# One encoder layer in float32: the first of the seven block products of the middle FFN pairs written as 512-column matmuls

## The chip, the cores and the metric

The kernel runs on one core of a Trainium2 chip. The metric is the device time of one execution in microseconds (us), as the median of several runs. A difference of about 0.2% (2.1 us) is what a measurement of this kernel can tell from none.

## The reference

One layer of a bidirectional encoder on 512 tokens of width 1024, all in float32. The change lies in the two feed-forward networks (FFN), one before and one after the attention part:

```python
def _swiglu(x, w_gate, w_up, w_down):
    return (jax.nn.silu(x @ w_gate) * (x @ w_up)) @ w_down

f = _swiglu(_rmsnorm(x, ffn1_pre_g[l]), ffn1_w_gate[l], ffn1_w_up[l], ffn1_w_down[l])
x = x + 0.5 * _rmsnorm(f, ffn1_post_g[l])
...   # attention branches, gates, output projection
f = _swiglu(_rmsnorm(x, ffn2_pre_g[l]), ffn2_w_gate[l], ffn2_w_up[l], ffn2_w_down[l])
x = x + 0.5 * _rmsnorm(f, ffn2_post_g[l])
```

`D_FF` is 2816, so each FFN has 22 blocks of 128 hidden features, and each block needs a piece of the gate weights and a piece of the up weights (a "pair").

## The kernel before

**Precision by splitting.** A float32 value is split into a high part `hi` (a cast to fp32r, done by ScalarE in line 113) and a low part `lo = x - hi` (VectorE, line 114). A product is the sum of high times high, high times low, and low times high: the helper `mm3` (lines 204 to 206) issues these as three matmuls.

**Seven products instead of eight.** For 20 of the 22 pairs of each FFN, `seven` computes the 2x2 block product (gate and up rows against two halves of 256 tokens, over two halves of the contraction) with seven block products after Strassen and Winograd. Product `i` of pair `j` multiplies a sum of weight blocks by a sum of token blocks; 1, 2 and 4 use the plain tokens (`hn` in the names), the others use sums (`v`). The products add up in three PSUM banks per pair: `q` takes 1, 6, 7 and 4, `p` takes 5 and 3, and `r` takes 2. A pair's products 7 and 4 are issued in the next pair's pass, so one pass over `j` issues: product 1 of `j`; 7 of `j-1` with 5 of `j`; then 2 and 6 of `j`, 4 of `j-1`, 3 of `j`.

**Narrow and wide.** A product has four contraction steps of 128. Narrow, it is 4 times `mm3` with 256 columns: twelve matmuls. Wide, the high weights multiply `[hi|lo]` of the tokens in one 512-column matmul per step (line 461), and the low weights multiply `hi` in one 256-column matmul per step (line 464): eight matmuls. High times low then lies in columns 256 to 511 of the bank and must be added to the rest by VectorE. `run` issues the 512-column halves of the products of one call first, then their 256-column halves. In each FFN, product 2 is wide for `j` from 4 to 16, and products 3, 5, 6, 7 and 4 in most pairs; product 1 is narrow everywhere.

**What follows a product.** After product 1, ScalarE copies `q[:, :256]` to `g` (line 495), from which the gate value of one token half is made; the same bank then goes on adding up products 6, 7 and 4. Line 506 on VectorE subtracts `q` (after product 7) from the copy `p5` of product 5, for the pair before; line 507 adds that sum's two halves; line 521 adds the two halves of `r` to `g`; line 536 subtracts the copy of `q` from `p`; line 638 multiplies gate and up. Lines 410 and 415 (`sums_of`) form weight sums for the next pair; lines 113 and 114 split the weight blocks.

**What sets the order.** TensorE's order inside `seven` is the order of the code, kept by manual dependencies. The order of VectorE and ScalarE is decided at build time by a scheduler with a model of its own. Each engine executes its list strictly in that order, and an instruction at the head of a list that waits on a semaphore holds all behind it.

Of the kernel before, what the change touches and what calls it, by code (L numbers as in the profile page):

```python
# [16 lines left out]
ALU = mybir.AluOpType  # L17
# [7 lines left out]
NF = 2816 // P  # L25
# [1 line left out]
EPS = 1e-6  # L27
NEG = -1.0e30
NUNIT = 38
WIDE = (5, 2, 6, 3, 7, 4)  # L30
PIECE = 1024
NPIECE = 6
SPREAD = 4
# [2 lines left out]
STD = 2  # L36
EARLY = 4
# [9 lines left out]
def block_kernel(ctx, tc, x, gains, weights, rpb_near, rpb_all, alibi0, alibi12, out):  # L47
    nc = tc.nc
# [12 lines left out]
    def unit(dt=F32, name="u"):  # L61
        return up.tile([P, 512], dt, tag="u", name=name)

    def twin(name):
        return up.tile([P, PIECE], F32R, tag="twin", name=name, bufs=8)
# [54 lines left out]
    state = {"used": False, "next": 0, "take": 0, "stop": EARLY + 2 * STD, "ahead": lambda: None}  # L120
# [231 lines left out]
    def combined():  # L352
# [17 lines left out]
        for n, of in ((5, lambda i: (whole[0][i], whole[1][i], sub)), (6, lambda i: (v[5][i], a[0][i], sub)),  # L370
# [5 lines left out]
            for i in range(2):  # L376
                if n in WIDE:
                    t = twin("v").rearrange("p (k s t) -> p k s t", k=2, s=2)
# [10 lines left out]
    def load_blocks(n0, j):  # L389

        w11, t1, t3 = unit(name="w11"), unit(name="t1"), unit(name="t3")
        gate, up = (n0 + j, n0 + EARLY + 2 * STD + j) if j < EARLY else [n0 + 2 * STD + 2 * j + i for i in range(2)]
        nc.sync.dma_start(t1, weights[up][:, :512])
        nc.sync.dma_start(t3, weights[up][:, :512])
        raw = {3: w11, 5: t1, 7: t3}
        if j < EARLY:
            raw[4] = unit(name="t4")
            nc.sync.dma_start(raw[4], weights[gate][:, 512:])
        else:
            r = wp.tile([P, PIECE], F32, tag="raw", name="raw", bufs=2)  # L400
            nc.sync.dma_start(r, weights[gate])
            raw[1], raw[2] = r[:, :512], r[:, 512:]
        nc.sync.dma_start(w11, weights[up][:, 512:])
        nc.gpsimd.dma_start(t1, weights[gate][:, :512], accum_op=ALU.add)  # L404
        nc.gpsimd.dma_start(t3, weights[up][:, 512:], accum_op=ALU.add)
        return raw

    def sums_of(raw):
        raw[6] = unit(name="t2")
        nc.vector.tensor_tensor(raw[6], raw[5], raw[3], op=ALU.add)  # L410
        if 4 in raw:
            nc.vector.tensor_tensor(raw[4], raw[6], raw[4], op=ALU.add)
        else:
            raw[4] = unit(name="t4")
            nc.vector.tensor_tensor(raw[4], raw[6], raw[2], op=ALU.add)

    def split_block(raw):
        w = wp.tile([P, PIECE], F32R, tag="w", name="w")
        split(w[:, :512], w[:, 512:], raw)
        return w  # L420

    def seven(use, mv, n_pairs, n0, behind, far, lead, raws, early, put, pin):

        blocks = {}
        o = {}

        def get(j):
            if j < n_pairs and j > 2:
                raws[j] = load_blocks(n0, j)
            if j >= n_pairs - 1:
                behind(far)

        def ready(j, i):
            if j < n_pairs:
                if j and loads:
                    loads.popleft()()  # L440
                if i == 1:
                    sums_of(raws[j])
                if j >= EARLY or i not in (1, 2):
                    blocks[j, i] = split_block(raws[j].pop(i))
            else:
                behind(lead)

        def product(j, i, key, start):
            if start:
                o[key, j] = bank(key)  # L450
            w = blocks.pop((j, i))
            high = [w[:, k * P:(k + 1) * P] for k in range(4)]
            low = [w[:, 512 + k * P:512 + (k + 1) * P] for k in range(4)]
            acc = o[key, j][:, :256]
            if i not in WIDE or j not in state["wide"] or (key in "qr" and j < EARLY) or (i == 2 and j > NF - STD - 4):
                for k in range(4):
                    mm3(acc, high[k], low[k], *mv[i][k][:2], start and k == 0, k == 3, skip_group_check=True)
                return
            for k in range(4):
                to = shaped(o[key, j], mv[i][k][2])  # L460
                nc.tensor.matmul(to, high[k], mv[i][k][2], start=start and k == 0, stop=False, skip_group_check=True)  # L461
            yield
            for k in range(4):
                nc.tensor.matmul(acc, low[k], mv[i][k][0], start=False, stop=k == 3, skip_group_check=True)  # L464

        def run(*products):
            products = [product(*p) for p in products]
            for _ in range(2):
                for p in products:
                    next(p, None)  # L470

        def full(j):
            return j in state["wide"] and j >= EARLY

        res = {}
        get(0)
        get(1)
        blocks[0, 5] = split_block(raws[0][5])
        ready(0, 1)
        raws[0].pop(5)  # L480
        for i in (6, 3, 7, 4):
            ready(0, i)
            if i == 3:
                put()
        begin = mark()
        for j in range(n_pairs + 1):
            now, was = j < n_pairs, j > 0
            get(j + 2)
            if now:
                if j < EARLY:  # L490
                    o["q", j], g = early[j]
                else:
                    run((j, 1, "q", True))
                    g = unit(name="g")
                    nc.scalar.copy(g[:, :256], o["q", j][:, :256])
                u = unit(name="up")
                res[j] = g, u, unit(name="p5") if j in state["wide"] else u[:, 256:]
            ready(j + 1, 1)
            if pin and j == 0:
                pool.append((pin, mark(), (mybir.EngineType.DVE,)))  # L500
            run(*[(j - 1, 7, "q", False)] * was, *[(j, 5, "p", True)] * now)
            if was:
                g0, u0, s0 = res.pop(j - 1)
                q0 = o["q", j - 1]
                if full(j - 1):
                    nc.vector.tensor_tensor(s0, s0, q0, op=ALU.subtract)
                    nc.vector.tensor_tensor(u0[:, 256:], s0[:, :256], s0[:, 256:], op=ALU.add)
                else:
                    nc.vector.tensor_tensor(u0[:, 256:], s0[:, :256], q0[:, :256], op=ALU.subtract)
                if j - 1 in state["wide"] and not full(j - 1):  # L510
                    nc.vector.tensor_tensor(u0[:, 256:], u0[:, 256:], s0[:, 256:], op=ALU.add)
            ready(j + 1, 5)
            if now:
                p = o["p", j]
                nc.scalar.copy(res[j][2], p if j in state["wide"] else p[:, :256])
            ready(j + 1, 2)
            two = now and j >= EARLY
            run(*[(j, 2, "r", True)] * two, *[(j, 6, "q", False)] * now, *[(j - 1, 4, "q", False)] * was, *[(j, 3, "p", False)] * now)
            if two:
                for part in range(1 + (full(j) and j <= NF - STD - 4)):  # L520
                    nc.vector.tensor_tensor(g[:, :256], g[:, :256], o["r", j][:, part * 256:part * 256 + 256], op=ALU.add)
            ready(j + 1, 6)
            if now:
                nc.scalar.copy(u if full(j) else u[:, :256], o["q", j] if full(j) else o["q", j][:, :256])
            ready(j + 1, 3)
            if was:
                if full(j - 1):
                    nc.scalar.copy(g0[:, 256:], q0[:, 256:])
                    nc.vector.tensor_tensor(g0[:, 256:], q0[:, :256], g0[:, 256:], op=ALU.add)
                    use(j - 1, g0, u0, g0[:, 256:])  # L530
                else:
                    use(j - 1, g0, u0, q0[:, :256])
            ready(j + 1, 7)
            if now:
                if full(j):
                    nc.vector.tensor_tensor(u, p, u, op=ALU.subtract)
                    nc.vector.tensor_tensor(u[:, :256], u[:, :256], u[:, 256:], op=ALU.add)
                else:
                    nc.vector.tensor_tensor(u[:, :256], p[:, :256], u[:, :256], op=ALU.subtract)
                if j in state["wide"] and not full(j):  # L540
                    nc.vector.tensor_tensor(u[:, :256], p[:, 256:], u[:, :256], op=ALU.add)
            ready(j + 1, 4)
        pool.append((begin, mark(), (mybir.EngineType.PE,)))
# [1256 lines left out]
```

## Time and profile before

| | |
|---|---|
| median of 3 runs | 1069.86 us (1069.64 to 1069.97) |
| profiled execution, its own time | 1070.8 us |
| span of that execution in the trace | 1069.0 us |
| granted TensorE clock | 0.998 |
| TensorE matmul busy | 1061.0 us (99% of the span), 5955 matmuls |
| VectorE busy | 871.1 us (81%) |
| ScalarE busy | 653.0 us (61%) |
| pairs `j` = 4 to 16 of the first FFN | about 72 to 200 us of the span |
| pairs `j` = 4 to 16 of the second FFN | about 798 to 925 us of the span |

The span is what the trace covers; the execution's own time is 1.8 us longer. Matmul records overlap (a 256-column matmul is recorded with 0.28 us, while the next one starts 0.12 us after it), so the time that a matmul costs is read from start to start. The same holds for VectorE's records: a 128x256 addition is recorded with 0.42 us, and the next one may start 0.33 us after its start.

### The profile page before, as it was taken

How to read it: one execution, taken by the hardware profiler on the slowest of the kernel's cores; microseconds unless marked ns; L12 is line 12 of the kernel's file. 1: busy time of each engine (PE TensorE's matmuls, PEld its weight loads, DVE VectorE, ACT ScalarE, POOL GpSimd, SP SyncE). 2: the span in 40 equal slices, each digit the busy share in tenths (PEclk: the TensorE clock that was granted, in tenths of full speed). 3: DMA queues.
4: the chain of work that ended last, by engine and by line, in shares of the span. 5: the costliest groups of instructions: out<-in, count | busy, mean ns of one | idle time of the engine just before them, and what ended most of it. 6: DMA issues, size and time to landing. Idle time of an engine off the chain costs nothing.

```text
span 1069.0 us, 17160 instructions
## 1 busy us (share of the span) xinstructions
PE 1061.0 (99%) x5955; PEld 926.4 (87%) x5955; DVE 871.1 (81%) x1694; ACT 653.0 (61%) x1348; POOL 193.1 (18%) x253
## 2 busy tenths in 40 slices
PE   9999999999999999999999999999999999999997
PEld 7898988998888988888988888889899899988886
DVE  7998999989987666676777644777998999989985
ACT  7656656566674655577766641366655566667671
POOL 4111211024334000000000001043311111124331
PEclk9999999999999999999999999999999999999999
DMA  9899987779993444322233239595947678869952
GB/s 331 188 231 234 235 206 200 197 182 264 248 311 118 154 158 164 116 68 74 80 89 97 79 106 308 148 199 186 286 100 197 158 198 204 216 203 234 217 195 79
DMA packets 98027, 193.95 MB, mean 181 GB/s; under 512 B 24338, under 2 KB 26898, under 8 KB 97939
## 3 DMA queue, kind: packets, MB, share of 16 engines
q1 hardware_dynamic: 69760, 138.37, 38.8%
q0 software_dynamic: 25488, 54.01, 28.3%
q8 instruction: 47, 0.77, 0.3%
q10 hardware_dynamic: 2690, 0.46, 0.2%
q14 instruction: 42, 0.34, 0.1%
HBM read 185.68 MB, written 9.68 MB: 183 GB/s over the span
## 4 chain that ended last, share of the span: by engine, by line
PE 92%; DMA 4%; DVE 2%; ACT 0%; issue 0%; SPq 0%; DVEq 0%; ACTq 0%
PE ps L204 10%; PE ps L206 10%; PE ps L205 10%; PE q L461 7%; PE q L206 6%; PE q L204 6%; PE q L205 6%; PE p L461 6%; PE q L464 4%; PE p L464 3%; PE c L206 2%; PE c L204 2%; PE c L205 2%; PE r L461 2%; PE r L204 1%; PE r L206 1%
## 5 line engine op out<-in xcount | busy, mean ns | idle before, releaser
L114 DVE TENSOR_TENSOR w<-raw,w 128x512 fp32r<-128x512 f32 (+1 forms) x142 | 129.8, 919 | 70.9 <-ACT w L113 68.2
L113 ACT CAST w<-t 128x512 fp32r<-128x512 f32 x160 | 98.0, 622 | 115.1 <-DVE t L410 62.6
L113 ACT CAST w<-raw 128x512 fp32r<-128x512 f32 (+1 forms) x142 | 114.1, 809 | 78.9 <-PE ps L205 31.9
L204 PE MATMUL ps<-hn,w 128*128 128x512 f32 (+1 forms) x360 | 136.5, 379 | 0.0
L206 PE MATMUL ps<-hn,w 128*128 128x512 f32 (+1 forms) x360 | 134.6, 374 | 0.0
L205 PE MATMUL ps<-hn,w 128*128 128x512 f32 (+1 forms) x360 | 134.3, 373 | 0.0
L114 DVE TENSOR_TENSOR w<-t,w 128x512 fp32r<-128x512 f32 x160 | 108.3, 685 | 1.0 <-ACT w L113 0.8
L404 POOL DMA_DIRECT2D t<-in_weights_dram x40 | 35.0, 875 | 286.1 <-DVE w L114 58.5
L206 PEld LDWEIGHTS ps<-hn,w 128*128 128x128 f32 x360 | 67.8, 188 | 12.7 <-DVE w L114 0.7
L204 PEld LDWEIGHTS ps<-hn,w 128*128 128x128 f32 x360 | 67.9, 189 | 11.4
L205 PEld LDWEIGHTS ps<-hn,w 128*128 128x128 f32 x360 | 67.9, 189 | 10.9
L461 PE MATMUL p<-v,w 128*128 128x512 f32 x272 | 73.1, 390 | 0.0
L113 ACT CAST w<-room 128x1024 fp32r<-128x1024 f32 x49 | 51.5, 1052 | 31.7 <-PE q L206 7.8
L114 DVE TENSOR_TENSOR w<-room,w 128x1024 fp32r<-128x1024 f32 x49 | 59.6, 1220 | 7.3 <-ACT w L113 4.1
L461 PE MATMUL q<-v,w 128*128 128x512 f32 x240 | 65.1, 392 | 0.0
L750 POOL DMA_DIRECT2D room<-in_weights_dram x7 | 6.1, 873 | 320.5 <-DMA room<-in_weights_dram 313.9
L461 PEld LDWEIGHTS p<-v,w 128*128 128x128 f32 x272 | 50.4, 188 | 10.2
L731 POOL DMA_DIRECT2D rows<-in_weights_dram x36 | 37.0, 1251 | 95.0 <-DVE w L114 61.6
L461 PEld LDWEIGHTS q<-v,w 128*128 128x128 f32 x240 | 43.0, 189 | 7.5
L113 ACT CAST w<-rows 128x512 fp32r<-128x512 f32 x62 | 36.0, 618 | 20.7 <-PE q L206 9.5
L206 PE MATMUL q<-hn,w 128*128 128x256 f32 x168 | 47.5, 283 | 0.0
L205 PE MATMUL q<-hn,w 128*128 128x256 f32 x168 | 47.5, 283 | 0.0
(334 smaller groups left out, 3066.0 us busy)
## 6 DMA issues: line engine op xcount, KB each, us to landing
raw<-in_weights_dram SPq DMA_DIRECT2D x94, 512.0 KB
t<-in_weights_dram SPq DMA_DIRECT2D x88, 256.0 KB
t<-in_weights_dram POOLq DMA_DIRECT2D x80, 256.0 KB, 5.7
room<-in_weights_dram SPq DMA_DIRECT2D x37, 512.0 KB
room<-in_weights_dram POOLq DMA_DIRECT2D x29, 512.0 KB, 11.9
w<-in_weights_dram SPq DMA_DIRECT2D x40, 256.0 KB
rows<-in_weights_dram POOLq DMA_DIRECT2D x36, 256.0 KB, 8.7
w<-in_weights_dram POOLq DMA_DIRECT2D x32, 256.0 KB, 9.1
```

Source lines behind the costliest of these rows:

```text
L113: nc.scalar.copy(hi, src)
L114: nc.vector.tensor_tensor(lo, src, hi.bitcast(F32), op=ALU.subtract)
L204: nc.tensor.matmul(o, sh, mh, start=start, stop=False, **kw)
L205: nc.tensor.matmul(o, sh, ml, start=False, stop=False, **kw)
L206: nc.tensor.matmul(o, sl, mh, start=False, stop=stop, **kw)
L404: nc.gpsimd.dma_start(t1, weights[gate][:, :512], accum_op=ALU.add)
L461: nc.tensor.matmul(to, high[k], mv[i][k][2], start=start and k == 0, stop=False, skip_group_check=True)
L464: nc.tensor.matmul(acc, low[k], mv[i][k][0], start=False, stop=k == 3, skip_group_check=True)
L731: nc.gpsimd.dma_start(u, block(*add, d)[:, cs], accum_op=ALU.add)
L750: nc.gpsimd.dma_start(to, self.block(*b, 0), accum_op=ALU.add)
```

## The change

Product 1 joins the wide products. Products 1 and 2 now share the condition that keeps the last three pairs narrow (`NF - STD - 4` is 16), and pairs below `EARLY` (4) compute product 1 elsewhere. So product 1 becomes wide for `j` = 4 to 16 in both FFNs, 26 products in all. Its high times low part now lies in `q[:, 256:]`; since `g` is copied from `q[:, :256]` only, VectorE adds the other half to `g` in a new instruction (line 497 of the changed kernel), on the same pairs. The change also moves later lines of the file by two: line 506 of before is line 508 after, 507 is 509, 521 is 523, 638 is 640.

```diff
-WIDE = (5, 2, 6, 3, 7, 4)
+WIDE = (1, 5, 2, 6, 3, 7, 4)
...
-            if i not in WIDE or j not in state["wide"] or (key in "qr" and j < EARLY) or (i == 2 and j > NF - STD - 4):
+            if i not in WIDE or j not in state["wide"] or (key in "qr" and j < EARLY) or (i in (1, 2) and j > NF - STD - 4):
                 for k in range(4):
                     mm3(acc, high[k], low[k], *mv[i][k][:2], start and k == 0, k == 3, skip_group_check=True)
                 return
...
                     run((j, 1, "q", True))
                     g = unit(name="g")
                     nc.scalar.copy(g[:, :256], o["q", j][:, :256])
+                    if full(j) and j <= NF - STD - 4:
+                        nc.vector.tensor_tensor(g[:, :256], g[:, :256], o["q", j][:, 256:], op=ALU.add)
```

On the three engines this gives the following. The names are tiles (`q`, `p`, `r` are PSUM banks, `w` split weights, `t` weight sums, `p_...` the copy `p5`); a row that ends in x4 stands for four instructions.

TensorE in pair 6 of the first FFN, before: the last two of the twelve matmuls of product 1, then products 7 and 5, product 2 (`r`), and the start of product 6 (the last row), with the engine whose semaphore a row waits for.

```order
L205 MATMUL q<-hn,w 128x256
L206 MATMUL q<-hn,w 128x256
L461 MATMUL q<-v,w 128x512 [waits Activation_49]
L461 MATMUL q<-v,w 128x512 x3
L461 MATMUL p<-v,w 128x512 x4
L464 MATMUL q<-v,w 128x256 x4
L464 MATMUL p<-v,w 128x256 x4
L461 MATMUL r<-hn,w 128x512 [waits PE_49]
L461 MATMUL r<-hn,w 128x512 x3
L461 MATMUL q<-v,w 128x512 [waits Activation_49]
```

The same place in the changed kernel.

```order
L461 MATMUL q<-hn,w 128x512 x4
L464 MATMUL q<-hn,w 128x256 x4
L461 MATMUL q<-v,w 128x512 [waits Activation_49]
L461 MATMUL q<-v,w 128x512 x3
L461 MATMUL p<-v,w 128x512 x4
L464 MATMUL q<-v,w 128x256 x4
L464 MATMUL p<-v,w 128x256 x4
L461 MATMUL r<-hn,w 128x512 [waits PE_49]
L461 MATMUL r<-hn,w 128x512 x3
L461 MATMUL q<-v,w 128x512 [waits DVE_49]
```

The twelve matmuls have become four of 512 and four of 256 columns; and the start of product 6, which writes into the bank that the new addition reads, now waits for VectorE where it waited for ScalarE.

VectorE in pair 6, before: from the multiplication of line 638 past the subtraction of line 506.

```order
L638 TENSOR_TENSOR h<-up,g 128x256 x2
L506 TENSOR_TENSOR p_1220<-p_1220,q 128x512
L410 TENSOR_TENSOR t_1347<-t_1195,w_1194 128x512
L507 TENSOR_TENSOR up<-p_1220 128x256
L415 TENSOR_TENSOR t_1349<-t_1347,raw 128x512
L114 TENSOR_TENSOR w<-t_1347,w 128x512
```

The same place in the changed kernel (lines 640, 508 and 509 are 638, 506 and 507 of before).

```order
L640 TENSOR_TENSOR h<-up,g 128x256 x2
L508 TENSOR_TENSOR p_1214<-p_1214,q 128x512
L410 TENSOR_TENSOR t_1338<-t_1192,w_1191 128x512
L497 TENSOR_TENSOR g<-g,q 128x256
L509 TENSOR_TENSOR up<-p_1214 128x256
L415 TENSOR_TENSOR t_1340<-t_1338,raw 128x512
L114 TENSOR_TENSOR w<-t_1338,w 128x512
```

The new addition stands behind the subtraction and the weight sum of line 410. It stands so in all even pairs from 6 to 16, in both FFNs.

VectorE in pair 7, before: from the split of a weight sum (line 114) past the subtraction of line 506.

```order
L114 TENSOR_TENSOR w<-t_1320,w 128x512
L410 TENSOR_TENSOR t_1470<-t_1320,w_1319 128x512
L114 TENSOR_TENSOR w<-raw,w 128x512
L638 TENSOR_TENSOR h<-up,g 128x256
L506 TENSOR_TENSOR p_1345<-p_1345,q 128x512
L415 TENSOR_TENSOR t_1472<-t_1470,raw 128x512
L114 TENSOR_TENSOR w<-t_1470,w 128x512
```

The same place in the changed kernel.

```order
L114 TENSOR_TENSOR w<-t_1314,w 128x512
L410 TENSOR_TENSOR t_1458<-t_1314,w_1313 128x512
L114 TENSOR_TENSOR w<-raw,w 128x512
L497 TENSOR_TENSOR g<-g,q 128x256
L640 TENSOR_TENSOR h<-up,g 128x256
L415 TENSOR_TENSOR t_1460<-t_1458,raw 128x512
L508 TENSOR_TENSOR p_1336<-p_1336,q 128x512
L114 TENSOR_TENSOR w<-t_1458,w 128x512
```

Here the new addition stands ahead of the multiplication, and the weight sum of line 415 has moved ahead of the subtraction. It stands so in the odd pairs from 7 to 15.

## The prediction

> **What bounds the kernel now.** I read the shares of busy time first, then the chain of waits, then TensorE's waits over the whole span, then stretches of one pair each. The page and TensorE's waits say:
>
> ```profile
> PE 1061.0 (99%) x5955; PEld 926.4 (87%) x5955; DVE 871.1 (81%) x1694; ACT 653.0 (61%) x1348; POOL 193.1 (18%) x253
> PE 92%; DMA 4%; DVE 2%; ACT 0%; issue 0%; SPq 0%; DVEq 0%; ACTq 0%
> PE warm L1577 <- DVE idle L1541: 1.2, 1, 1.2
> PE q L461 <- DVE p L506: 0.3, 1, 0.3
> PE q L270 <- ACT hn L330: 0.2, 1, 0.2
> ```
>
> TensorE carries the chain, and in the whole span it waits three times, 1.7 us in all. So time taken from TensorE's list comes off the end, and any wait put into it is added in full; no later wait can swallow it. Next, busy time by pair (columns PE, PEld, DVE, ACT, POOL, granted clock, DMA): two pairs of the first FFN, and in the second FFN the last pair with product 2 wide and the first with it narrow.
>
> ```profile
> 108.25:118.05 9.80, 9.80 (x62) 8.81 (x61) 8.95 (x20) 4.36 (x10) 1.77 (x2) 1.00 0.93 217
> 118.05:127.85 9.80, 9.80 (x62) 8.82 (x61) 9.40 (x18) 7.66 (x17) 1.77 (x2) 1.00 0.94 240
> 916.91:926.71 9.80, 9.80 (x61) 8.81 (x61) 9.40 (x20) 6.02 (x14) 1.75 (x2) 1.00 0.70 163
> 926.71:936.56 9.85, 9.85 (x65) 9.03 (x65) 8.71 (x18) 6.41 (x14) 1.75 (x2) 1.00 0.98 291
> ```
>
> A pair costs TensorE 9.80 us without a gap, at full clock. VectorE has 18.35 of 19.60 us filled in two pairs: 1.25 us are free, before anything is added. ScalarE has room. The whole case therefore turns on two questions: what wide saves on TensorE, and where in VectorE's list the new addition stands.
>
> **What the wide form saves.** TensorE's rows in pair 8 of the first FFN (start, length, line; product 1's first and last of twelve matmuls, and then 7, 5, their low parts, 2, 6):
>
> ```profile
> 110.19 0.64 PE L464 MATMUL r<-hn,w 128*128 128x256 f32 x4
> 112.11 0.28 PE L204 MATMUL q<-hn,w 128*128 128x256 f32 x1
> 113.43 0.28 PE L206 MATMUL q<-hn,w 128*128 128x256 f32 x1
> 113.55 1.09 PE L461 MATMUL q<-v,w 128*128 128x512 f32 x4
> 114.48 1.07 PE L461 MATMUL p<-v,w 128*128 128x512 f32 x4
> 115.39 0.64 PE L464 MATMUL q<-v,w 128*128 128x256 f32 x4
> 115.86 0.64 PE L464 MATMUL p<-v,w 128*128 128x256 f32 x4
> 116.34 1.09 PE L461 MATMUL r<-hn,w 128*128 128x512 f32 x4
> 117.27 1.07 PE L461 MATMUL q<-v,w 128*128 128x512 f32 x4
> ```
>
> Narrow, product 1 takes 113.55 - 112.11 = 1.44 us, 0.12 per matmul. Wide, four of 512 columns behind narrow ones take 114.48 - 113.55 = 0.93, and four of 256 take 115.86 - 115.39 = 0.47: 1.40 together. The columns streamed are the same, and only 0.04 us goes. The stretches agree: the pair in which product 2 turns narrow is 9.85 - 9.80 = 0.05 longer. I take 0.04, since it comes from product 1's own place; ends 0 and 0.05. Twenty-six products: **-1.0 us** (0 to -1.3). The Trainium skill (TensorE: Matmul & The Clock Gate, Back-to-back issue gap) gives an isolated warm matmul N/2.4 ns plus 2.5 ns; by that, as an estimate, a product would save only 4 x 2.5 = 0.01 us and the 26 together 0.3, so the rule leaves even less than the rows do.
>
> **What the addition costs.** The nearest row is the same operation on another bank:
>
> ```profile
> L521 DVE TENSOR_TENSOR g<-g,r 128x256 f32<-128x256 f32 x24 | 10.1, 420 | 6.4 <-PE r L464 5.4
> ```
>
> It takes 0.42 us to its end. The row also shows that VectorE waits there for product 2, so VectorE starts each pair's round in step with TensorE, when `r` is done. From there I follow its list. These rows run from pass 7's line 521 to pair 8's line 507 (the eight rows between the second and third are back to back), and the slot in which the new addition will stand is that of line 507:
>
> ```profile
> 110.87 0.42 DVE L521 TENSOR_TENSOR g<-g,r 128x256 f32<-128x256 f32 x1 [0.85 <-PE r L464]
> 111.21 0.42 DVE L638 TENSOR_TENSOR h<-up,g 128x256 f32<-128x256 f32 x1
> ...
> 115.55 0.75 DVE L638 TENSOR_TENSOR h<-up,g 128x256 f32<-128x256 f32 x2
> 116.22 0.68 DVE L506 TENSOR_TENSOR p<-p,q 128x512 f32<-128x512 f32 x1
> 116.81 0.69 DVE L410 TENSOR_TENSOR t<-t,w 128x512 f32<-128x512 f32 x1
> 117.42 0.42 DVE L507 TENSOR_TENSOR up<-p 128x256 f32<-128x256 f32 x1
> ```
>
> *Even pairs.* Every even pair from 6 to 16 has the addition behind lines 506 and 410. It starts at 117.42 and ends at 117.84. Product 6 writes the bank that the addition reads, so it must wait; TensorE wants to start it at 117.27, and with product 1 shorter, at 117.23. It is late by 117.84 - 117.23 = 0.61 us. What a wait on VectorE costs beyond its end, this trace shows once, in the pair at 88 us, where product 4 waited for line 506:
>
> ```profile
> 87.32 1.07 PE L461 MATMUL q<-v,w 128*128 128x512 f32 x4
> 87.92 0.68 DVE L506 TENSOR_TENSOR p<-p,q 128x512 f32<-128x512 f32 x1
> 88.65 0.77 PEld L461 LDWEIGHTS q<-hn,w 128*128 128x128 f32 x4 [0.68 <-DVE p L506]
> 88.65 1.20 PE L461 MATMUL q<-hn,w 128*128 128x512 f32 x4 [0.26 <-DVE p L506]
> 89.68 1.07 PE L461 MATMUL p<-v,w 128*128 128x512 f32 x4
> ```
>
> Line 506 ended at 88.60, and the product after the waiting one started at 89.68, 1.08 later, where four wide matmuls otherwise take 0.91 (114.48 to 115.39). So the wait costs 0.17 more: 0.05 for the signal and 0.12 because the weight load had waited too (PEld starts with the matmul). The Trainium skill (TensorE: Matmul & The Clock Gate, the table at its head) says that TensorE's queue pulls weight loads ahead of matmuls in flight; here the load did not pass the wait. Were it to pass, an even pair would lose 0.12 less.
>
> An even pair thus loses 0.61 + 0.17 = 0.78 us. There are six in each FFN: 12 x 0.78 = **+9.4 us**. Low end: no shift of product 6 (0.57) and the signal alone (0.05), 12 x 0.62 = 7.4; high end: another 0.1 from VectorE's own slips, 10.6. Does VectorE still start in step? Before the line 521 at 110.87 it waits 0.85 us, and pair 7's addition takes 0.33 of that: yes, so the loss recurs and does not die out. Queued behind the addition on VectorE are line 507 and the weight splits for the next pair, 0.33 later; no one waits for those within this pair, since TensorE is 0.78 late itself, and line 521 waits for `r` again.
>
> *Odd pairs.* Here the addition stands early, ahead of product 6 by more than a microsecond, but it and the moved line 415 now precede line 506, for which product 4 waits. From pass 8's line 521 to pair 9's product 4, VectorE and then TensorE:
>
> ```profile
> 120.67 0.88 DVE L521 TENSOR_TENSOR g<-g,r 128x256 f32<-128x256 f32 x2
> 125.86 0.42 DVE L638 TENSOR_TENSOR h<-up,g 128x256 f32<-128x256 f32 x1
> 126.19 0.68 DVE L506 TENSOR_TENSOR p<-p,q 128x512 f32<-128x512 f32 x1
> 126.79 0.68 DVE L415 TENSOR_TENSOR t<-t,raw 128x512 f32<-128x512 f32 x1
> 127.98 0.39 PE L461 MATMUL q<-hn,w 128*128 128x512 f32 x1
> ```
>
> Addition 125.86, line 638 at 126.19, line 415 at 126.52, line 506 from 127.12 to 127.80. Product 4 is due at 127.98 - 0.04 = 127.94. With 0.05 for the signal it is just in time, but its weight load, which starts some 0.2 before the matmul, is late by about 0.1: I put 0.03 on it. Ten such places (odd pairs 7 to 15 in both FFNs): **+0.3 us** (0 to 1.3, at 0.13 each).
>
> *First pairs.* The wait at 88.65 lies in pair 5 of the first FFN, behind its own new addition: 0.33 longer. In pair 4 the addition takes the slot of line 509:
>
> ```profile
> 77.02 0.42 DVE L509 TENSOR_TENSOR up<-up,q 128x256 f32<-128x256 f32 x1
> 77.45 1.09 PE L461 MATMUL q<-v,w 128*128 128x512 f32 x4
> ```
>
> It ends at 77.44, product 6 is due at 77.41: 0.03 + 0.17 = 0.20. Together **+0.5 us** (0 to 0.7).
>
> **Sum.** 9.4 + 0.3 + 0.5 - 1.0 = +9.2 us on the profiled execution's 1070.8 us, which is 0.9 above the median of the runs. On the median, 1069.86, it gives **1079.1 us**, 0.9% slower. All low ends with the full saving: 7.4 - 1.3 = +6.1, 1076.0. All high ends: 10.6 + 1.3 + 0.7 - 0 = +12.6, 1082.5. A difference of 0.2% (2.1 us) is what a measurement can tell from none.
>
> **The rivals.**
>
> *The addition is hidden.* VectorE has 1.25 us free in two pairs and the additions need 2 x 0.33. If VectorE came to line 506 in the even pairs 0.6 us earlier than in the trace, or TensorE's wait for the addition never bit, only the saving would be left: 1069.86 - 1.0 = 1068.8, no change that can be told. Its point of decision is the end of the addition at 117.23. Against it: the free time lies in front of line 521, where VectorE waits for `r`; work after it cannot be moved into it, and the rows from 110.87 to 117.42 leave no gap.
>
> *VectorE becomes the bound.* If its waits did not shrink, two pairs would grow by 2 x 0.33 = 0.66 with thirteen additions per FFN, 26 x 0.33 = 8.6 us: 1078.5. The time is almost the forecast's, but TensorE would wait for weight splits (line 114) everywhere, and VectorE would show no wait at line 521. Against it: 0.85 us of waiting at 110.87 is more than the 0.33 added.
>
> *Both products wait.* If a ScalarE copy or a split slips in the odd pairs, line 506 passes product 4's due time with its full delay, and a third of a microsecond is lost in those too: 10 x 0.33 = 3.3 in place of 0.3, 1082.1. For it: the margin there is only 0.1 us.
>
> **How the numbers follow.** The forecast has 0.72, the hidden addition 0.10 (0.02 of that for a saving over 2.1 us, which nothing above supports), VectorE as the bound 0.10, both products waiting 0.08. Slower is the sum of three, 0.90; same 0.08; faster 0.02. The range takes in the forecast's bounds and the second rival and the third's centre, with a little below for waits that come out smaller: 1075.5 to 1083.0; the hidden addition is left out.
>
> **What would show it.** In the changed kernel's trace: twelve waits of TensorE for the new addition, 0.5 to 0.7 us each, at the start of product 6 in pairs 6, 8, ... 16 of both FFNs; product 1 in 1.40 us from first to next; odd pairs of 9.76 to 9.8 us and even ones of about 10.5; line 521 still waiting for `r` in both. I am wrong if VectorE's new addition ends before TensorE is done with product 2, or if TensorE's waits name another line.

## The result and the profile after

The changed kernel takes 1080.49 us (median of 6 runs, 1080.06 to 1085.46); the kernel before, on the same chip, 1069.91 us (median of 6, 1069.35 to 1070.81). The ratio is 1.0106 with a 95% interval of 1.0094 to 1.0117: about 1% slower, where 1079.1 us (+9.2) was forecast. The profiled execution took 1080.23 us with a span of 1078.4, which is 9.4 longer than the span of before.

First the shares of busy time, then TensorE's waits and those of its weight loads for lines 497 and 508 over the whole span (engine, tile and line, what was waited for; then us in total, times, longest):

```profile
PE 1064.2 (99%) x5851; PEld 918.4 (85%) x5851; DVE 878.4 (81%) x1720; ACT 653.7 (61%) x1348; POOL 187.1 (17%) x253
PE q L461 <- DVE g L497: 5.8, 12, 0.5
PE q L461 <- DVE p L508: 0.5, 1, 0.5
PEld q L461 <- DVE g L497: 11.0, 12, 0.9
PEld q L461 <- DVE p L508: 3.1, 11, 1.0
```

There are 26 more instructions on VectorE and 104 fewer on TensorE. The new line is waited for twelve times, as forecast. TensorE's share is 99% as before: the shares tell nothing of the loss.

TensorE in pair 8 of the first FFN (start, length, line): products 1 (two rows), 7, 2, 6, 4, and the start of pair 9's product 1:

```profile
112.46 1.09 PE L461 MATMUL q<-hn,w 128*128 128x512 f32 x4
113.39 0.63 PE L464 MATMUL q<-hn,w 128*128 128x256 f32 x4
113.86 1.09 PE L461 MATMUL q<-v,w 128*128 128x512 f32 x4
...
116.67 1.09 PE L461 MATMUL r<-hn,w 128*128 128x512 f32 x4
118.24 1.20 PE L461 MATMUL q<-v,w 128*128 128x512 f32 x4 [0.48 <-DVE g L497]
119.28 1.08 PE L461 MATMUL q<-hn,w 128*128 128x512 f32 x4
...
123.03 1.09 PE L461 MATMUL q<-hn,w 128*128 128x512 f32 x4
```

Product 1 takes 113.86 - 112.46 = 1.40 us. Product 6 was due 0.93 after product 2's start, at 117.60, and starts at 118.24, 0.64 late; product 4 behind it starts 1.04 later where 0.91 is usual, 0.13 more. Together 0.77 us are lost. The wait is listed as 0.48 only, since it counts from the recorded end of product 2 (116.67 + 1.09 = 117.76), which lies 0.16 behind the point at which the next product could have started. The pass takes 123.03 - 112.46 = 10.57 us.

VectorE over the same place, the slot before product 6 and the two starts in step with `r`:

```profile
111.22 0.42 DVE L523 TENSOR_TENSOR g<-g,r 128x256 f32<-128x256 f32 x1 [0.53 <-PE r L464]
...
116.57 0.68 DVE L508 TENSOR_TENSOR p<-p,q 128x512 f32<-128x512 f32 x1
117.17 0.69 DVE L410 TENSOR_TENSOR t<-t,w 128x512 f32<-128x512 f32 x1
117.77 0.41 DVE L497 TENSOR_TENSOR g<-g,q 128x256 f32<-128x256 f32 x1
118.10 0.42 DVE L509 TENSOR_TENSOR up<-p 128x256 f32<-128x256 f32 x1
...
121.79 0.88 DVE L523 TENSOR_TENSOR g<-g,r 128x256 f32<-128x256 f32 x2 [0.86 <-PE r L464]
```

The addition ends at 118.18 and product 6 starts at 118.24. VectorE then waits for `r` again, now in both of the two pairs (0.53 and 0.86 us).

The stretches from the start of product 1 in pair 4 to its start in pair 17, one per FFN (the columns are from:to, length, then busy time by engine, PE, PEld, DVE, ACT, POOL, granted clock, DMA share and GB/s), before and after:

```profile
72.24:200.31 128.07, 127.81 (x791) 114.95 (x789) 118.06 (x231) 77.16 (x166) 24.76 (x28) 1.00 0.87 218
797.60:925.11 127.51, 127.51 (x791) 115.02 (x790) 117.26 (x231) 76.47 (x164) 22.80 (x26) 1.00 0.75 185
```

```profile
71.60:204.82 133.22, 129.69 (x738) 111.09 (x737) 121.78 (x244) 77.33 (x166) 24.81 (x29) 1.00 0.84 211
802.49:934.54 132.05, 129.16 (x738) 111.16 (x737) 120.63 (x243) 76.57 (x164) 22.84 (x26) 1.00 0.72 180
```

The two stretches grow by 5.15 and 4.54, 9.69 us in all. The rest of the span holds only -0.3: the first stretch starts 0.64 earlier, the part between is 0.38 longer, and the end is the same. So the whole difference lies where the change is, at full clock.

### The profile page after: what moved, and what is told of

Read it like the earlier page. It is cut to its first block, busy times and chain, and to the rows that moved or that the text cites. A ratio compares the mean times of both kernels' runs of the same rounds, so it can differ in the third digit from the quotient of the medians.

```text
span 1078.4 us, 17006 instructions
## 1 busy us (share of the span) xinstructions
PE 1064.2 (99%) x5851; PEld 918.4 (85%) x5851; DVE 878.4 (81%) x1720; ACT 653.7 (61%) x1348; POOL 187.1 (17%) x253
## 4 chain that ended last, share of the span: by engine, by line
PE 83%; DVE 13%; issue 2%; ACT 1%; DMA 1%; POOL 0%; DVEq 0%; ACTq 0%; POOLq 0%
PE ps L204 10%; PE ps L206 10%; PE ps L205 10%; PE q L461 8%; PE q L204 5%; PE q L206 5%; PE q L205 5%; DVE w L114 5%; PE p L461 4%; PE q L464 3%; PE c L206 2%; PE c L205 2%; PE c L204 2%; PE p L464 2%; PE r L205 1%
## 5 line engine op out<-in xcount | busy, mean ns | idle before, releaser
L461 PE MATMUL q<-hn,w 128*128 128x512 f32 x224 | 61.2, 395 | 0.6 <-DVE p L508 0.5
L733 POOL DMA_DIRECT2D rows<-in_weights_dram x36 | 34.6, 1168 | 97.6 <-DMA room<-in_weights_dram 52.8
L461 PEld LDWEIGHTS q<-hn,w 128*128 128x128 f32 x224 | 39.5, 189 | 9.5 <-DVE p L508 3.1
```

The lines of the kernel that those rows point to most:

```text
L733: nc.gpsimd.dma_start(u, block(*add, d)[:, cs], accum_op=ALU.add)
```

## Experiments

My theory: the time is lost because the addition stands behind two other instructions in VectorE's list and product 6 cannot write the bank before it has been read. Rivals: VectorE's added work by itself; the wide form by itself; and, as a question of size, whether a wait costs more than its lateness. Seven kernels separate these; each was compared with the kernel before on the same chip.

### The read of the bank without the wide form

The kernel before, with product 1 narrow, and an instruction of the same size at the same place in the code that reads `q` (the maximum of `g` and the part of the bank from which `g` was copied, so the values stay as they are).

```diff
                     nc.scalar.copy(g[:, :256], o["q", j][:, :256])
+                    if full(j) and j <= NF - STD - 4:
+                        nc.vector.tensor_tensor(g[:, :256], g[:, :256], o["q", j][:, :256], op=ALU.max)
```

> The kernel before, product 1 narrow everywhere, plus one VectorE instruction per pair at the place of the new addition: g = max(g, q[:, :256]), which leaves g as it is. Same length of work, and it reads the bank of q, so product 6 must wait for it. Theory (place in VectorE's list): the twelve waits come with it and only the saving is missing: 12 x 0.78 + 0.3 + 0.5 = +10.2 us over before. Rival 1 (VectorE's added work is what costs): 26 x 0.33 = +8.6 us, with TensorE waiting for weight splits. Rival 2 (the wide form itself is slow at this place): no change.

Measured: 1080.57 us (4 runs), ratio 1.0095 (1.0082 to 1.0109), +10.5. TensorE's waits:

```profile
PE q L461 <- DVE g L497: 5.8, 13, 0.5
```

The whole loss is there with all of product 1's matmuls as before. The wide form is not needed for it. Of the thirteen waits twelve are in the even pairs from 6 on, as in the changed kernel; the thirteenth is in pair 4 of the first FFN, where line 410, ahead of the new instruction on VectorE, had waited 0.99 us for a DMA transfer (0.18 in the changed kernel).

### The same work on VectorE without the bank

```diff
+                    if full(j) and j <= NF - STD - 4:
+                        nc.vector.tensor_tensor(g[:, :256], g[:, :256], g[:, :256], op=ALU.max)
```

> As e1, but the instruction is g = max(g, g): the same work at the same place of VectorE's list (in even pairs behind the subtraction of line 506 and the weight sum of line 410), with no read of the bank, so that nothing of TensorE waits for it. Theory: no waits at product 6; only the first pairs and the odd pairs may lose a little, 0 to +0.8 us over before. Rival 1 (the work): +8.6 us as in e1. Rival 2 (wide form): no change.

Measured: 1070.09 us (11 runs), ratio 0.9998 (0.9989 to 1.0006). TensorE does not wait for any bank in this trace, and the stretches are no longer than before (the first is 0.52 shorter, since the wait of pair 5 in the trace of before does not come here):

```profile
72.35:199.90 127.55, 127.55 (x790) 115.02 (x789) 121.21 (x243) 77.49 (x166) 24.80 (x28) 1.00 0.87 218
797.07:924.60 127.53, 127.53 (x790) 115.01 (x789) 120.33 (x243) 76.50 (x164) 22.86 (x26) 1.00 0.73 183
```

VectorE is busy for 121.21 and 120.33 us, about as long as in the changed kernel (121.78 and 120.63), and it costs nothing. VectorE's work as the bound falls. In the even pairs the added instruction stands behind lines 508 and 410 in both kernels, so there the two experiments together leave the read of the bank. In the odd pairs the build put line 415 behind 508 here and ahead of it in the kernel with the read, so these two do not separate what the odd pairs lose.

### The wide form with the bank read by ScalarE

The changed kernel, but ScalarE's copy takes the whole bank to `g`, and VectorE adds the two halves of the copy. Product 6 then waits for ScalarE alone, as it did before.

```diff
-                    nc.scalar.copy(g[:, :256], o["q", j][:, :256])
-                    if full(j) and j <= NF - STD - 4:
-                        nc.vector.tensor_tensor(g[:, :256], g[:, :256], o["q", j][:, 256:], op=ALU.add)
+                    both_halves = full(j) and j <= NF - STD - 4
+                    nc.scalar.copy(g if both_halves else g[:, :256], o["q", j] if both_halves else o["q", j][:, :256])
+                    if both_halves:
+                        nc.vector.tensor_tensor(g[:, :256], g[:, :256], g[:, 256:], op=ALU.add)
```

> The changed kernel, but ScalarE copies the whole bank of q to g after product 1 (128x512 where it copied 128x256), and VectorE adds the two halves of g, without reading the bank. VectorE's list keeps its order in the even pairs. Product 6 then waits for ScalarE alone, whose copy is done more than 2 us before. Theory: the waits go and the saving of the wide form stays: -1.0 + 0.3 for the first pair = -0.7 us against before (0 to -1.3). Rival 1 (the work): +8.6 us. Rival 2 (wide form slow): about +10 us.

Measured: 1070.23 us (11 runs), ratio 0.9998 (0.9989 to 1.0007): no difference from before that the runs show. TensorE waits for no bank. The longer copy, 576 ns, finds its place on ScalarE without idle time before it: the first row below is its group in pairs 6 to 16 of the first FFN. Under it stand the stretches, which together are the shortest of the kernels that compute everything:

```profile
L496 ACT COPY g<-q 128x512 f32<-128x512 f32 x11 | 6.3, 576 | 0.0
```

```profile
71.87:198.94 127.07, 127.07 (x739) 112.07 (x737) 121.11 (x243) 80.25 (x166) 24.85 (x28) 1.00 0.88 219
796.65:923.75 127.10, 127.10 (x738) 112.04 (x737) 120.47 (x243) 79.55 (x164) 22.87 (x26) 1.00 0.74 183
```

Against the narrow form without a wait (127.55 and 127.53), thirteen wide products save 0.48 and 0.43 us, 0.035 each. That is the saving of the wide form in the traces, 0.9 us for 26; the medians do not resolve it.

### The addition moved ahead, by two slots and by one

The changed kernel with manual dependencies that put VectorE's lines 508 and 410 of a pass behind the pass's addition. A second kernel moves only line 410, so that in the even pairs the addition stands behind line 508 alone. The notes behind `#` are not in the code. In these kernels the addition is line 505 and the wide matmuls are line 462.

```diff
+        def behind_added(j, n=-1):
+            if j in added:
+                tc.add_manual_dep(nc.cur_bb.bb.instructions[n], added[j], ...)
...
                         nc.vector.tensor_tensor(g[:, :256], g[:, :256], o["q", j][:, 256:], op=ALU.add)
+                        added[j] = nc.cur_bb.bb.instructions[-1].name
...
         nc.vector.tensor_tensor(raw[6], raw[5], raw[3], op=ALU.add)    # line 410
+        then()                                                         # behind_added(j - 1)
...
                     nc.vector.tensor_tensor(s0, s0, q0, op=ALU.subtract)   # line 508
+                    behind_added(j)                                        # in the first kernel alone
```

> The changed kernel with VectorE's order fixed in one point: the subtraction of line 506 and the weight sum of line 410 must stand behind the new addition of the same pass. In the even pairs the addition then comes 0.60 + 0.60 = 1.2 us earlier and ends 0.6 us before product 6 is due. Nothing else changes. Theory: no waits for the addition: -1.0 + 0.3 = -0.7 us against before (0 to -1.3). Rival 1 (the work): +8.6 us whatever the order. Rival 2 (wide form slow): about +10 us.

> The changed kernel with only the weight sum of line 410 forced behind the new addition. In the even pairs the addition then stands right behind the subtraction of line 506, 0.60 us earlier than in the changed kernel, and ends just when product 6 is due. Theory, with a wait costing its lateness plus 0.17 us for signal and weight load: 12 x (0.00 + 0.17) = 2.0, - 1.0 for the wide form, + 0 to 0.5 for the first pairs: +1.0 to +1.5 us over before. If a wait costs its lateness alone: -1.0 to -0.5. If the place does not matter and the work does: +8.6.

Measured, first kernel: 1070.66 us (11 runs), ratio 1.0004 (0.9995 to 1.0012). The wait is gone but for one place, pair 4 of the first FFN, where product 6 is late; with it the two stretches are 0.76 us longer than with ScalarE's copy (254.93 against 254.17):

```profile
PE q L462 <- DVE g L505: 0.5, 1, 0.5
```

Second kernel: 1072.14 us (9 runs, two of them above 1075), ratio 1.0026 (1.0016 to 1.0036), +2.2 where 1.0 to 1.5 was expected. TensorE's waits have no row for the bank, those of its weight loads have one, and another for ScalarE's copy of `p`:

```profile
PEld q L462 <- DVE g L505: 3.8, 12, 0.3
PEld p L462 <- ACT p L526: 0.4, 1, 0.4
```

In the timeline, products 2, 6, 4 and 3 of pair 8, the next product's start, and the addition on VectorE:

```profile
115.70 1.09 PE L462 MATMUL r<-hn,w 128*128 128x512 f32 x4
116.68 1.19 PE L462 MATMUL q<-v,w 128*128 128x512 f32 x4
117.70 1.09 PE L462 MATMUL q<-hn,w 128*128 128x512 f32 x4
118.63 1.09 PE L462 MATMUL p<-v,w 128*128 128x512 f32 x4
119.56 0.64 PE L465 MATMUL r<-hn,w 128*128 128x256 f32 x4
```

```profile
116.21 0.41 DVE L505 TENSOR_TENSOR g<-g,q 128x256 f32<-128x256 f32 x1
```

The addition ends at 116.62, just as product 6 is due (115.70 + 0.93 = 116.63). Yet product 4 starts at 117.70 where it was due at 117.54: 0.16 us are lost to a wait that is not late at all. The two products behind it take 0.93 each; in the kernel with ScalarE's copy, whose list on TensorE is the same, they take 0.90 and 0.91:

```profile
117.08 1.07 PE L461 MATMUL q<-hn,w 128*128 128x512 f32 x4
117.98 1.07 PE L461 MATMUL p<-v,w 128*128 128x512 f32 x4
118.89 0.64 PE L464 MATMUL r<-hn,w 128*128 128x256 f32 x4
```

That is 0.05 more, 0.21 in all in pair 8. From product 1 to the next product 1, eleven of the twelve even passes are 0.16 to 0.21 longer than with ScalarE's copy. The twelfth, pair 14 of the first FFN, is 0.45 longer: there product 3's first weight load waited for ScalarE's copy of `p` besides. The stretches agree: against that kernel's 127.07 and 127.10 they are 1.37 and 1.10 longer, 2.47 together.

```profile
72.14:200.58 128.44, 128.44 (x738) 111.36 (x737) 122.16 (x244) 77.16 (x166) 24.81 (x28) 1.00 0.86 219
798.41:926.61 128.20, 128.20 (x739) 111.45 (x737) 121.28 (x244) 76.36 (x164) 22.87 (x26) 1.00 0.72 182
```

Against the stretches of before, 128.07 and 127.51, they are 0.37 and 0.69 longer, 1.1 together, and that is within what was expected. Profiled execution against profiled execution the kernel is 1.5 slower (1072.32 against 1070.8). On the medians it is 2.2, since the profiled execution of before stands 0.8 above the median of these runs.

### The addition moved back

The changed kernel with the addition written after `ready(j + 1, 1)`, which forms the weight sums, and held behind line 415. Here the addition is line 501 and the wide matmuls are line 462.

```diff
-                        nc.vector.tensor_tensor(g[:, :256], g[:, :256], o["q", j][:, 256:], op=ALU.add)
...
             ready(j + 1, 1)
+            if now and full(j) and j <= NF - STD - 4:
+                nc.vector.tensor_tensor(g[:, :256], g[:, :256], o["q", j][:, 256:], op=ALU.add)
+                tc.add_manual_dep(nc.cur_bb.bb.instructions[-1], state["sum"], ...)    # line 415
```

> The changed kernel with the addition forced behind the weight sum of line 415. In the even pairs it stands 0.33 + 0.60 = 0.93 us later than in the changed kernel (behind lines 506, 410, 507, 415), and in the odd pairs behind 638 and 415, where it ends at 127.21 in the trace of before, against 127.03 when product 6 is due. Theory: even pairs 12 x (0.61 + 0.93 + 0.17 = 1.71) = 20.5; odd pairs 10 x (0.18 + 0.17) = 3.5; first pairs 1.1 + 0.6; saving -1.0: +24.7 us over before (22 to 26), with 24 or 25 waits for the addition. If the work decides: +8.6, as in the changed kernel.

Measured: 1095.65 us (4 runs), ratio 1.0239 (1.0226 to 1.0252), +25.7. TensorE's wait, and in the timeline products 2, 6 and 4 of pair 8 and the addition on VectorE:

```profile
PE q L462 <- DVE g L501: 19.4, 21, 1.4
```

```profile
119.17 1.09 PE L462 MATMUL r<-hn,w 128*128 128x512 f32 x4
121.69 1.19 PE L462 MATMUL q<-v,w 128*128 128x512 f32 x4 [1.42 <-DVE g L501]
122.72 1.08 PE L462 MATMUL q<-hn,w 128*128 128x512 f32 x4
```

```profile
121.22 0.41 DVE L501 TENSOR_TENSOR g<-g,q 128x256 f32<-128x256 f32 x1
```

The addition ends at 121.63, 1.53 behind the due time of 120.10; product 4 starts at 122.72, due at 121.01: 1.71 lost. There are 21 listed waits where 24 to 25 were expected. Product 6 is late in all twelve even pairs and all ten odd ones (in these it starts 1.24 to 1.25 behind product 2 in place of 0.93), and in pair 4 of the first FFN: 23 places. The list puts one of the odd ones down to ScalarE and leaves out another; pairs 4 and 5 have the one wait and not two or three. The total is 1.0 above the expected sum and inside its range; the odd pairs alone lose 0.7 more than expected, 0.42 each where it was 0.35.

### The wide form without the addition

The changed kernel with the two new lines under the copy taken out. It leaves the high times low part of product 1 out of one token half's gate values.

> The changed kernel without the new addition: the high times low part of product 1 is left out of the gate of one token half. What is left is the wide form alone, with VectorE's work as before. Theory: 26 x 0.04 = -1.0 us against before (0 to -1.3), at the limit of what the runs can tell; product 1 in 1.40 us from first to next in the trace, and no waits at product 6. If the wide form itself were slow at this place: up to +10 us.

Measured: 1070.18 us (11 runs), ratio 1.0003 (0.9994 to 1.0012). The expected gain of 1.0 us is not in the medians; the interval reaches from 0.6 us faster to 1.3 slower. The stretches, 127.10 and 127.08 us, are those of the kernel with ScalarE's copy. So the most that the change could have brought is the 0.9 us read there, and the runs, which spread over 3 us in this kernel (1068.73 to 1072.00), do not show it.

## Why the prediction was right

| even pair, product 6 | addition ends, against product 6's due time | lost, read at product 4 | whole kernel against before |
|---|---|---|---|
| addition first | 0.6 ahead | 0 | +0.6 (-0.5 to +1.3) |
| behind line 508 | 0.0 | 0.16 | +2.2 |
| behind 508 and 410 (the change) | 0.58 late | 0.77 | +10.6 |
| behind 508, 410, 509 and 415 | 1.53 late | 1.71 | +25.7 |

**The even pairs.** Forecast 0.61 late, 0.17 on top, 0.78 lost, twelve times. Measured in pair 8: the addition ends 0.58 late, 0.19 on top, 0.77 lost, twelve waits. The table shows both parts of the term: a slot more or less on VectorE moves the loss by its length, and about 0.17 remain even at no lateness. The place in VectorE's list is the cause, and it is shown by kernels that change the order and leave the work as it is. The prediction named waits of 0.5 to 0.7 us; the list has 0.48 for each, for the reason given with the timeline.

**The odd pairs.** Forecast 0.03 each, 0.3 in all. The weight loads' row for line 508 counts eleven places, ten odd pairs and pair 5, and product 4 of pair 9 takes 130.00 - 129.07 = 0.93 in place of 0.91:

```profile
102.65 1.09 PE L461 MATMUL q<-hn,w 128*128 128x512 f32 x4
...
129.07 1.09 PE L461 MATMUL q<-hn,w 128*128 128x512 f32 x4
130.00 1.07 PE L461 MATMUL p<-v,w 128*128 128x512 f32 x4
```

So 0.02 there, and nine of the ten odd passes take 9.79 to 9.82 us from product 1 to product 1. An odd and an even pass together, pair 7's and pair 8's, are 20.38 us (product 1 at 102.65 to product 1 at 123.03), against 19.60 before: +0.78, where 0.78 + 0.03 - 2 x 0.04 = 0.73 was forecast.

The tenth, pair 11 of the first FFN, takes 10.16. Two rows of VectorE, then products 6, 4 and 3:

```profile
144.00 0.69 DVE L538 TENSOR_TENSOR up<-p,up 128x512 f32<-128x512 f32 x1 [0.38 <-ACT w L113]
...
148.96 0.68 DVE L508 TENSOR_TENSOR p<-p,q 128x512 f32<-128x512 f32 x1
```

```profile
148.51 1.07 PE L461 MATMUL q<-v,w 128*128 128x512 f32 x4
149.69 1.20 PE L461 MATMUL q<-hn,w 128*128 128x512 f32 x4
150.72 1.07 PE L461 MATMUL p<-v,w 128*128 128x512 f32 x4
```

Line 538 had waited 0.38 us for a split on ScalarE, and line 508 ends at 149.64, 0.22 behind the 149.42 at which product 4 was due. From product 6 to product 3 it takes 2.21 where 1.82 is usual: 0.39 lost, more than the 0.3 forecast for all ten. The order that puts lines 497 and 415 ahead of 508 in the odd pairs was not tested by itself.

**The first pairs.** Forecast +0.5: 0.33 in pair 5 and 0.20 in pair 4 of the first FFN. Pair 5's came:

```profile
86.60 1.11 PE L461 MATMUL q<-v,w 128*128 128x512 f32 x4
88.24 1.19 PE L461 MATMUL q<-hn,w 128*128 128x512 f32 x4 [0.53 <-DVE p L508]
```

Product 4 starts 88.24 - 86.60 = 1.64 behind product 6, where it was 88.65 - 87.32 = 1.33: 0.31 more. Pair 4's did not come: the addition ends at 76.56 there, 0.21 before product 6 is due at 76.77.

**The saving.** Forecast 0.04 per product, 1.0 in all; the traces show 0.035 and 0.9. It was right in size, but only the traces show it.

**The sum.** +9.2 on the span, measured +9.4. By places, the forecast with the saving of 0.04 taken off for each product, the measured growth from product 1 to the next product 1 in the traces before and after (the forecast adds up to 9.1 here by rounding):

| | forecast, us | measured, us |
|---|---|---|
| twelve even pairs | +8.9 | +9.1 |
| ten odd pairs | -0.1 | +0.4 |
| pairs 4 and 5 | +0.3 | +0.2 |
| rest of the span | 0 | -0.3 |

The even pairs carry the forecast, and there it is right in place, number and size. That the sum comes so close is partly luck: the odd pairs cost 0.5 more than forecast, and the first pairs and the rest of the span, whose -0.3 I cannot place, take most of it back.

On the medians the difference is 10.6, 1.4 more than forecast. 1.2 of that is no step of the mechanism: the profiled execution of before stood 0.9 above the median of its runs, and that of after 0.3 below (1080.23 against 1080.49). I had carried the span's sum over to the median as it was, and a scatter of about 1 us per run goes into that step.

**The rivals.** *The addition is hidden* would have been right with the addition two slots earlier: its named point of decision, the end of the addition against product 6's due time, is what the table varies. *VectorE becomes the bound* fell twice: VectorE's group for line 523 shows more waiting for `r` in the same window of 120 us (9.1 against 6.4 us), and the same work without the bank cost nothing that the runs show.

```profile
L523 DVE TENSOR_TENSOR g<-g,r 128x256 f32<-128x256 f32 x24 | 10.1, 419 | 9.1 <-PE r L464 8.9
```

*Both products wait* came in one of the ten odd pairs, pair 11 of the first FFN, and by the slip on ScalarE that it named; in the other nine the margin of product 4 held.

## What to carry to other kernels

Before an instruction that reads a PSUM bank is added, look for who writes that bank next and where the reader lands in its engine's list: here the 26 added instructions cost nothing that could be told where no matmul waited for them, and up to 1.71 us a pair where one did. If the bank is already read early by another engine, let that engine take the whole bank and do the rest on the copy; here this took the price from 10.6 us to nothing that can be told. And merging narrow matmuls into wide ones of the same total columns is worth only what start-to-start times of both forms show, here 0.035 us per product of twelve matmuls.

## What the runs showed that I had not expected

A wait that is over exactly when the matmul is due still cost time: in the kernel with the addition behind line 508 alone, the addition ended at 116.62, product 6 was due at 116.63, and 0.16 us went. The first weight load of the product had waited with it: it started at 116.67 with the matmul, where with ScalarE's copy it starts 0.23 us ahead (115.94 and 116.17). Such a wait has no row among TensorE's own waits, only among those of its weight loads (3.8 us in 12). The two products after it took up to 0.93 us each in place of 0.90 and 0.91; why they do is not settled. Where both have a row, TensorE's understates the loss: 5.8 us in twelve waits, 12 x 0.77 = 9.2 lost.
